# Attention of a decoder step: values' product as rounded 512-column passes, fused score step, reordered sample step

## The chip, the cores and the metric

One core of a Trainium2 chip. Time is device time in microseconds (us) of one execution; the kernel before has a median of 2323.82 us over 3 runs (2323.4 to 2323.91).

## The reference

One layer of a hybrid decoder for a prompt of 2048 tokens and for 8 sample rows with one token each. All arrays are float32, the width is 1024.

```python
proj = h @ w_in                       # h = x * (1 + scale) + shift
u_s, z_s, q, k, v, z_a, g_s, g_a = split(proj)
# prompt attention: blocks of 128 queries, keys of the own block and the one before
s = einsum('bnqkgd,bnskd->bnkgqs', qb, kk) * 64 ** -0.5 + rel_bias   # masked: -1e30
m = max(s.max(-1), sinks)
p = exp(s - m) / (exp(s - m).sum(-1) + exp(sinks - m))
o = einsum('bnkgqs,bnskd->bnqkgd', p, vv)
# sample attention: the same for one query per row against 128 cached keys and its own
...
b_a = (o * silu(z_a)) @ w_branch_a    # and an SSM branch b_s, a gated merge, w_out, LayerNorm
```

There are 16 heads of 64 and 4 key/value heads; four heads share one. `sinks` is one extra score per head that has no value.

## The kernel before

Every large product is done at nearly full precision with three passes of TensorE in a rounded float32 type (fp32r): each operand is split into a rounded high part and the low rest, and high x high, high x low and low x high are added (line 78). `products` goes through output blocks of 128 columns (jobs); a job is five chunks of the tokens (512, 256, 512, 264 and 512 columns in the order ORD), each with 24 matmuls into one of three PSUM accumulators `acc`. ScalarE copies an accumulator out (`zr`, L586) and writes it to DRAM (`zsD`, `gsD`, `gaD`).

Beside the jobs runs a side generator. A call after the third, sixth and eighth k of each chunk (a tick) issues its next piece. The instructions that result are put in order on each engine by the framework, which runs a model of the engines while it builds the program; each engine then works its queue in that order, and waits where an input or a buffer isn't ready.

The attention is such a side generator, beside 18 jobs. `attn_setup` (beside one job) writes the table of relative biases to DRAM (`biasD`, 3 MB, L894) and does the 8 sample rows: scores batch by batch (L924 transposes the cached keys, L930 multiplies), a softmax over 129 columns, transposes (L937, L938) and the product with the values: per batch a matmul over the 128 cached keys (L949) and one over the own key (L950), in one of four groups of 32 output columns (`tile_position`). `attn_blocks` (beside up to 17 jobs) runs 2 halves of the heads (P) x 16 blocks of 128 queries through a pipeline: a block starts each 7 ticks (`ii`) and goes through one stage per tick:

- `load` (SyncE's DMA queue), `conv` (splits q and k into high and low; q's parts lie above each other so that one pass does both);
- `scores` twice: matmuls into `ps` (L1034), then one VectorE step, score x 0.125 + bias, into `t1` (L1036);
- `soft` twice: row maximum (L868), with the sink (L869), negated (L871), exponential with a row sum on ScalarE (L876), sum, reciprocal, scaling (L881);
- `trans` twice: 8 transposes of p on TensorE into `pt` (L1048) and copies to SBUF (L1050);
- `pv` and `out`: o from float32 matmuls with 64-column weights of v (L1061), the halves e = 0 and 1 into partitions 0 to 63 and 64 to 127 of `po`; copy (L1068), times silu(z_a) on POOL (L1069), write to DRAM.

At the kernel's start the adaptive projection (L185) also works in column groups of 32, here with four groups taken in turn (0, 2, 1, 3).

PSUM has eight banks: three accumulators, two `ps`, two `pt`, one `po`. For a float32 matmul the trace has two records, for one in fp32r and for a transpose one. The next phase begins when all jobs are done.

Of the kernel before, what the change touches and what calls it, by code (L numbers as in the profile page):

```python
# [39 lines left out]
class Trunk:  # L40
# [842 lines left out]
    def attn_setup(self, p, pp):  # L883
# [7 lines left out]
        fr = p.tile([16, 384], F32, name="fr")  # L891
        nc.vector.memset(fr, NEG)
        nc.vector.tensor_copy(fr[:, 127:256], pr)
# [27 lines left out]
        for b in range(NS):  # L921
# [9 lines left out]
            yield  # L931
# [3 lines left out]
        yield  # L935
# [10 lines left out]
        for b in range(NS):  # L946
            i, n = divmod(b, 4)
            r = slice(32 * n, 32 * n + 32)
            nc.tensor.matmul(po[r, i], pT[:, b], vc[:, b], start=True, stop=False, tile_position=(0, 32 * n))  # L949
            nc.tensor.matmul(po[r, i], pl[:, b], vn[:, b], start=False, stop=True, tile_position=(0, 32 * n))  # L950
# [22 lines left out]
    def attn_blocks(self, p, pp, ii):  # L973
# [6 lines left out]
        sk = p.tile([128, 16], F32, name="skb", bufs=1)  # L980
        for P in range(2):
            v.tensor_copy(sk[:, 8 * P:8 * P + 8].rearrange("p (s i) -> p s i", s=2),
                          sn[:, 8 * P:8 * P + 8].rearrange("p (i s) -> p s i", s=2))
# [5 lines left out]
        def load(s):  # L989
            P, blk = s["P"], s["blk"]  # L990
            ts = slice(128 * blk, 128 * blk + 128)
            if blk == 0:
                bias = cur["bias"] = p.tile([128, 8, 384], F32, name="bias", bufs=1)
                for i in range(4):
                    for e in range(2):
                        src = self.biasD[8 * P + 2 * i + e, 127:127 + 383 * 128].rearrange("(i l) -> i l", l=383)
                        nc.sync.dma_start(bias[:, 4 * e + i, 0:256], src[:, 0:256])
                        nc.sync.dma_start(bias[:, 4 * e + i, 256:384], src[:, 0:128])
# [8 lines left out]
            vf = p.tile([128, 128], F32, name="vf", bufs=3)  # L1007
            nc.sync.dma_start(vf, self.vD[ts, P * 128:(P + 1) * 128])
            old = cur.get("v")
            s["v"] = (vf, old) if blk % 2 == 0 else (old, vf)  # L1010
            cur["v"] = vf
# [14 lines left out]
        def scores(s, e):  # L1026
            kw, qs = s["kw"], s["q"][e]
            b0 = 0 if s["blk"] % 2 else 128
            t1 = s["t", e] = p.tile([128, 4, 256], F32, name="t1", bufs=3)
            for g in range(2):  # L1030
                ps = pp.tile([128, 2, 256], F32, name="ps", bufs=2)
                for a2 in range(2):
                    for i, kk in enumerate((kh, kl)):
                        nc.tensor.matmul(ps[:, a2, kw], qs[:, 2 * g + a2], kk[:, g, kw], start=(i == 0), stop=(i == 1))  # L1034
                hd = slice(4 * e + 2 * g, 4 * e + 2 * g + 2)
                v.scalar_tensor_tensor(t1[:, 2 * g:2 * g + 2, kw], ps[:, :, kw], 0.125, s["bias"][:, hd, b0:b0 + kw.stop],  # L1036
                                       op0=OP.mult, op1=OP.add)

        def soft(s, e):
            mx = p.tile([128, 4], F32, name="mx")  # L1040
            g4 = 4 * (2 * s["P"] + e)
            self.softmax(p, s["t", e], mx, sk[:, g4:g4 + 4], 4, s["kw"])

        def trans(s, e):
            for h in s["hs"]:
                pt = pp.tile([128, 4, 128], F32, name="pt", bufs=2)
                for a in range(4):
                    nc.tensor.transpose(pt[:, a], s["t", e][:, a, h * 128:(h + 1) * 128], self.ident)  # L1048
                s["pT", e, h] = p.tile([128, 4, 128], F32, name="pT", bufs=4)
                nc.scalar.copy(s["pT", e, h], pt)  # L1050

        def pv(s):
            s["po"] = pp.tile([128, 4, 128], F32, name="po", bufs=1)
            s["z4"] = p.tile([128, 4, 128], F32, name="z4")
            nc.sync.dma_start(s["z4"], self.zaP[s["P"]][:, :, s["blk"] * 128:(s["blk"] + 1) * 128].rearrange("a p n -> p a n"))
            hs = s["hs"]
            for g in range(2):
                a = slice(2 * g, 2 * g + 2)
                for h in hs:
# [338 lines left out]
```

## Time and profile before

| | |
|---|---|
| median of 3 runs | 2323.82 us |
| the profiled execution | 2322.61 us, its span 2320.8 us |
| TensorE (PE) busy | 2271.6 us, 98% of the span |
| VectorE (DVE) | 1394.5 us, 60% |
| ScalarE (ACT) | 755.2 us, 33% |
| GpSimd (POOL) | 347.2 us, 15% |
| sample step | about 905 to 970 us from the span's start |
| attention blocks | about 985 to 1490 us |

Matmuls are pipelined: a record's duration is modelled and longer than the distance from one start to the next, which is what it costs. PEld is the weight load, which overlaps the matmuls. In a row, "idle before" is the time that the engine stood still ahead of the group, with what ended it.

### The profile page before, as it was taken

What the parts mean: (1) busy time and instruction counts of PE and PEld (TensorE: products, weight loads), DVE (VectorE), ACT (ScalarE), POOL (GpSimd) and SP (SyncE); (2) the same over time, 40 slices, a digit from 0 to 9 for tenths busy, and PEclk for the clock granted to TensorE, in tenths of its full rate; (3) what the DMA queues carried; (4) which work ended last, traced back from release to release, by engine and by line L of the source; (5) the groups of instructions that cost most, each with busy time, mean ns of one, the idle gap of its engine ahead of it and who ended that gap; (6) DMA issues with size and microseconds to landing.
All of it is one profiled execution on the core that took longest, in us unless ns stands there. A gap on an engine that the chain in (4) does not pass through costs nothing.

```text
span 2320.8 us, 34854 instructions
## 1 busy us (share of the span) xinstructions
PE 2271.6 (98%) x12819; PEld 1898.6 (82%) x12819; DVE 1394.5 (60%) x3100; ACT 755.2 (33%) x1636; POOL 347.2 (15%) x420
## 2 busy tenths in 40 slices
PE   7999999999999999999999999999999999999997
PEld 5888898888888888687877888887877888888886
DVE  4896229998888872167776666426446114224887
ACT  3411213331111211156676555435225113212100
POOL 1100001111112110000010000013552000222232
PEclk9999999999999999999999999999999999999999
DMA  9344623344434335633344333448337547667431
GB/s 293 104 150 127 202 77 113 110 124 117 117 115 119 115 112 129 132 105 110 103 140 116 91 105 111 114 111 221 116 103 241 148 124 219 197 183 239 147 114 65
DMA packets 387499, 317.97 MB, mean 137 GB/s; under 512 B 89334, under 2 KB 331406, under 8 KB 385743
## 3 DMA queue, kind: packets, MB, share of 16 engines
q1 hardware_dynamic: 349616, 260.28, 39.6%
q10 hardware_dynamic: 37712, 55.47, 7.0%
q8 instruction: 101, 1.65, 0.3%
q14 instruction: 70, 0.57, 0.1%
HBM read 195.24 MB, written 122.63 MB: 137 GB/s over the span
## 4 chain that ended last, share of the span: by engine, by line
PE 80%; DMA 8%; DVE 4%; SPq 3%; issue 2%; ACT 2%; POOL 1%; POOLq 0%; DVEq 0%; ACTq 0%
PE acc L78 56%; PE po L1332 7%; PE po L1061 3%; PE ps L1034 3%; PE pt L1048 2%; DMA z<-zsD 2%; PE acc L665 2%; DMA biasD<-fr 2%; PE xp L784 1%; PE yp L817 1%; PE yp L816 1%; SPq L178 1%; DVE sg L1197 1%; DMA xst<-ozP 1%; DMA xst<-ysD 1%
## 5 line engine op out<-in xcount | busy, mean ns | idle before, releaser
L78 PE MATMUL acc<-hh,whi 128*128 128x512 f32 (+2 forms) x2000 | 713.5, 357 | 0.1
L78 PE MATMUL acc<-hl,whi 128*128 128x512 f32 (+2 forms) x2000 | 703.6, 352 | 0.0
L78 PE MATMUL acc<-hh,wlo 128*128 128x512 f32 (+2 forms) x2000 | 701.8, 351 | 0.2 <-DVE wlo L59 0.2
L78 PEld LDWEIGHTS acc<-hh,whi 128*128 128x128 f32 x2000 | 377.3, 189 | 54.7 <-issue 8.5
L78 PEld LDWEIGHTS acc<-hl,whi 128*128 128x128 f32 x2000 | 377.5, 189 | 54.2 <-issue 8.0
L78 PEld LDWEIGHTS acc<-hh,wlo 128*128 128x128 f32 x2000 | 377.2, 189 | 52.1 <-issue 5.3
L78 PE MATMUL acc<-xh,whi 128*128 128x512 f32 (+2 forms) x960 | 335.9, 350 | 12.7 <-ACT sg L1192 10.4
L78 PE MATMUL acc<-xl,whi 128*128 128x512 f32 (+2 forms) x960 | 334.9, 349 | 1.9 <-DVE xl L1139 1.8
L78 PE MATMUL acc<-xh,wlo 128*128 128x512 f32 (+2 forms) x960 | 333.2, 347 | 0.0
L78 PEld LDWEIGHTS acc<-xh,whi 128*128 128x128 f32 x960 | 181.5, 189 | 41.1 <-ACT sg L1192 15.1
L78 PEld LDWEIGHTS acc<-xl,whi 128*128 128x128 f32 x960 | 181.4, 189 | 26.5 <-DVE xl L1139 4.0
L78 PEld LDWEIGHTS acc<-xh,wlo 128*128 128x128 f32 x960 | 181.3, 189 | 23.0
L59 DVE TENSOR_TENSOR wlo<-wst,whi 128x1024 fp32r<-128x1024 f32 x74 | 96.3, 1301 | 100.6 <-ACT whi L58 99.8
L1139 DVE TENSOR_TENSOR xl<-xst,xh 128x1024 fp32r<-128x1024 f32 (+2 forms) x84 | 104.2, 1257 | 81.3 <-ACT xh L1138 81.1
L876 ACT ACTIVATE t<-t,nm 128x256 f32<-128x256 f32 (+1 forms) x256 | 125.8, 495 | 33.0 <-DVE nm L871 30.2
L1036 DVE SCALAR_TENSOR_TENSOR t<-ps,bias 128x512 f32<-128x512 f32 (+1 forms) x128 | 81.8, 670 | 86.0 <-PE ps L1034 79.1
L58 ACT CAST whi<-wst 128x1024 fp32r<-128x1024 f32 x74 | 77.7, 1050 | 156.1 <-PE acc L78 140.6
L1069 POOL TENSOR_TENSOR o<-o,z 128x512 f32<-128x512 f32 x32 | 42.7, 1336 | 539.3 <-ACT o L1068 513.1
L1138 ACT CAST xh<-xst 128x1024 fp32r<-128x1024 f32 (+2 forms) x84 | 86.0, 1045 | 104.9 <-DMA xst<-mD 32.7
L586 ACT COPY zr<-acc 128x512 f32<-128x512 f32 (+2 forms) x120 | 59.9, 499 | 164.3 <-PE acc L78 132.1
L1332 PE MATMUL po<-wol,xh 128*128 128x512 f32 (+1 forms) x272 | 102.7, 377 | 0.8 <-DVE wol L1255 0.8
L1332 PE MATMUL po<-woh,xl 128*128 128x512 f32 (+1 forms) x272 | 102.6, 377 | 0.0
(355 smaller groups left out, 3277.8 us busy)
## 6 DMA issues: line engine op xcount, KB each, us to landing
wst<-in_w_in SPq DMA_DIRECT2D x50, 512.0 KB
uD<-u ACTq DMA_DIRECT2D x8, 1088.0 KB
u<-uD SPq DMA_DIRECT2D x32, 272.0 KB
yD<-y ACTq DMA_DIRECT2D x64, 132.0 KB
x<-in_x_prompt SPq DMA_DIRECT2D x16, 512.0 KB
wa<-in_w_ada SPq DMA_DIRECT2D x16, 512.0 KB
qf<-qD SPq DMA_DIRECT2D x32, 256.0 KB
z<-zaP SPq DMA_DIRECT2D x32, 256.0 KB
```

What stands on the lines that cost most here:

```text
L58: nc.scalar.copy(hi, st)
L59: nc.vector.tensor_tensor(lo, st, hi, op=OP.subtract)
L78: self.nc.tensor.matmul(ps[:, :n], w[:, k, :], x[:, k, :], start=(k == 0 and i == 0), stop=(k == KT - 1 and i == 2))
L586: nc.scalar.copy(z[:, :n], ps[:, :n])
L665: nc.tensor.matmul(ps[:mt, :256], x[:, k, ts], w[:, k, :], start=(i == 0), stop=(i == 23))
L876: nc.scalar.activation(t1[:, h, kw], t1[:, h, kw], AF.Exp, bias=nm[:, h:h + 1], accum_out=den[:, h:h + 1])
L1034: nc.tensor.matmul(ps[:, a2, kw], qs[:, 2 * g + a2], kk[:, g, kw], start=(i == 0), stop=(i == 1))
L1036: v.scalar_tensor_tensor(t1[:, 2 * g:2 * g + 2, kw], ps[:, :, kw], 0.125, s["bias"][:, hd, b0:b0 + kw.stop], op0=OP.mult, op1=OP.add)
L1061: nc.tensor.matmul(s["po"][e * 64:(e + 1) * 64, a], s["v"][h][:, g * 64:(g + 1) * 64], s["pT", e, h][:, a], start=(h == hs[0]), stop=(h == ...
L1138: nc.scalar.copy(xv(hi[:, k - 1:k + 1]), sv(st))
L1139: nc.vector.tensor_tensor(xv(lo[:, k - 1:k + 1]), sv(st), xv(hi[:, k - 1:k + 1]), op=OP.subtract)
L1332: nc.tensor.matmul(ps[:, :w], X[a][:, k, ts], Wo[h * w // 512][b][:, k, ws], start=(i == 0), stop=(i == 23))
```

## The change

The product with the values takes p as a rounded high and a low part (`ph`, `pl`) and v as high and low parts side by side in 128 weight columns (`vs`); a pass gives high rows in partitions 0 to 63 of `po` and low rows in 64 to 127, for all four heads of a key/value head at once (512 columns). A copy and two additions put them together in `o4`. The stages now go by key/value head (g) and not by half (e); the pipeline has twelve stages, `ii` stays 7. Score, bias and the row's maximum with the sink (as a minimum of the negated scores) are one VectorE instruction, `tensor_tensor_reduce`; its scale is -0.125, so the bias table is stored times 8 and the exponential has scale -1. In the sample step scores come two batches per tick, the softmax has four ticks, and the product goes over the four column groups in turn, all cached keys first and then the own ones.

```diff
         pr = pp.tile([16, 129], F32, name="pt", bufs=2)
         nc.tensor.matmul(pr, rb, oh, start=True, stop=True)
         fr = p.tile([16, 384], F32, name="fr")
+
         nc.vector.memset(fr, NEG)
-        nc.vector.tensor_copy(fr[:, 127:256], pr)
+        nc.vector.tensor_scalar(fr[:, 127:256], pr, 8.0, None, op0=OP.mult)
         nc.sync.dma_start(self.biasD.rearrange("h (r l) -> h r l", l=384), fr[:, None, :].to_broadcast([16, 128, 384]))
 
...
             for P in range(2):
                 i = b * 2 + P
                 nc.tensor.matmul(ss, qm[:, i * 128:(i + 1) * 128], kt[:, P], start=(i == 0), stop=(i == 15))
-            yield
+            if b % 2:
+                yield
         nc.vector.scalar_tensor_tensor(t1[:, 0], ss, 0.125, t1[:, 0], op0=OP.mult, op1=OP.add)
         mx = p.tile([128, 1], F32, name="mxs")
         self.softmax(p, t1, mx, sk, 1, slice(0, 129))
-        yield
+        for _ in range(4):
+            yield
...
         po = pp.tile([128, 2, 256], F32, name="po", bufs=1)
-        for b in range(NS):
-            i, n = divmod(b, 4)
-            r = slice(32 * n, 32 * n + 32)
-            nc.tensor.matmul(po[r, i], pT[:, b], vc[:, b], start=True, stop=False, tile_position=(0, 32 * n))
-            nc.tensor.matmul(po[r, i], pl[:, b], vn[:, b], start=False, stop=True, tile_position=(0, 32 * n))
+        yield
+        for i in range(2):
+            for pm, vm, first in ((pT, vc, True), (pl, vn, False)):
+                for n in range(4):
+                    b = 4 * i + n
+                    nc.tensor.matmul(po[32 * n:32 * n + 32, i], pm[:, b], vm[:, b], start=first, stop=not first,
+                                     tile_position=(0, 32 * n))
...
-        sk = p.tile([128, 16], F32, name="skb", bufs=1)
+        nsk = p.tile([128, 16], F32, name="skb", bufs=1)
         for P in range(2):
-            v.tensor_copy(sk[:, 8 * P:8 * P + 8].rearrange("p (s i) -> p s i", s=2),
-                          sn[:, 8 * P:8 * P + 8].rearrange("p (i s) -> p s i", s=2))
+            v.tensor_scalar(nsk[:, 8 * P:8 * P + 8].rearrange("p (g e a) -> p g e a", g=2, e=2),
+                            sn[:, 8 * P:8 * P + 8].rearrange("p (g a e) -> p g e a", g=2, e=2), -1.0, None, op0=OP.mult)
 
...
                     for e in range(2):
                         src = self.biasD[8 * P + 2 * i + e, 127:127 + 383 * 128].rearrange("(i l) -> i l", l=383)
-                        nc.sync.dma_start(bias[:, 4 * e + i, 0:256], src[:, 0:256])
-                        nc.sync.dma_start(bias[:, 4 * e + i, 256:384], src[:, 0:128])
+                        nc.sync.dma_start(bias[:, 4 * (i // 2) + 2 * e + i % 2, 0:256], src[:, 0:256])
+                        nc.sync.dma_start(bias[:, 4 * (i // 2) + 2 * e + i % 2, 256:384], src[:, 0:128])
...
             for h in range(2):
                 nc.sync.dma_start(s["kf"][h * 64:(h + 1) * 64], self.kD[P][:, ts].rearrange("(g d) n -> d g n", g=2))
-            vf = p.tile([128, 128], F32, name="vf", bufs=3)
-            nc.sync.dma_start(vf, self.vD[ts, P * 128:(P + 1) * 128])
-            old = cur.get("v")
-            s["v"] = (vf, old) if blk % 2 == 0 else (old, vf)
-            cur["v"] = vf
+            s["vf"] = p.tile([128, 2, 64], F32, name="vf", bufs=1)
+            nc.sync.dma_start(s["vf"], self.vD[ts, P * 128:(P + 1) * 128].rearrange("t (g d) -> t g d", g=2))
 
...
+            vs = p.tile([128, 2, 128], F32R, name="vs", bufs=3)
+            nc.scalar.copy(vs[:, :, 0:64], s["vf"])
+            v.tensor_tensor(vs[:, :, 64:128], s["vf"], vs[:, :, 0:64], op=OP.subtract)
+            old = cur.get("v")
+            s["v"] = (vs, old) if s["blk"] % 2 == 0 else (old, vs)
+            cur["v"] = vs
+
+        def scores(s, g):
+
+            kw = s["kw"]
             b0 = 0 if s["blk"] % 2 else 128
-            t1 = s["t", e] = p.tile([128, 4, 256], F32, name="t1", bufs=3)
-            for g in range(2):
+            t1 = s["t", g] = p.tile([128, 4, 256], F32, name="t1", bufs=3)
+            nm = s["nm", g] = p.tile([128, 4], F32, name="nm", bufs=3)
+            for e in range(2):
                 ps = pp.tile([128, 2, 256], F32, name="ps", bufs=2)
                 for a2 in range(2):
                     for i, kk in enumerate((kh, kl)):
-                        nc.tensor.matmul(ps[:, a2, kw], qs[:, 2 * g + a2], kk[:, g, kw], start=(i == 0), stop=(i == 1))
-                hd = slice(4 * e + 2 * g, 4 * e + 2 * g + 2)
-                v.scalar_tensor_tensor(t1[:, 2 * g:2 * g + 2, kw], ps[:, :, kw], 0.125, s["bias"][:, hd, b0:b0 + kw.stop],
-                                       op0=OP.mult, op1=OP.add)
-
-        def soft(s, e):
-            mx = p.tile([128, 4], F32, name="mx")
-            g4 = 4 * (2 * s["P"] + e)
-            self.softmax(p, s["t", e], mx, sk[:, g4:g4 + 4], 4, s["kw"])
-
-        def trans(s, e):
+                        nc.tensor.matmul(ps[:, a2, kw], s["q"][e][:, 2 * g + a2], kk[:, g, kw], start=(i == 0), stop=(i == 1))
+                for a2 in range(2):
+                    h = 2 * e + a2
+                    hs = 8 * s["P"] + 4 * g + h
+                    v.tensor_tensor_reduce(t1[:, h, kw], ps[:, a2, kw], s["bias"][:, 4 * g + h, b0:b0 + kw.stop], -0.125,
+                                           nsk[:, hs:hs + 1], OP.add, OP.min, nm[:, h:h + 1])
+
+        def soft(s, g):
+            kw, nm, t1 = s["kw"], s["nm", g], s["t", g]
+            hs = 8 * s["P"] + 4 * g
+            es = p.tile([128, 4], F32, name="es")
+            v.tensor_tensor(es, nm, nsk[:, hs:hs + 4], op=OP.subtract)
+            den = p.tile([128, 4], F32, name="den")
+            for h in range(4):
+                nc.scalar.activation(t1[:, h, kw], t1[:, h, kw], AF.Exp, bias=nm[:, h:h + 1], scale=-1.0,
+                                     accum_out=den[:, h:h + 1])
+            nc.scalar.activation(es, es, AF.Exp)
+            v.tensor_tensor(den, den, es, op=OP.add)
+            v.reciprocal(den, den)
+            for h in range(4):
+                v.tensor_scalar(t1[:, h, kw], t1[:, h, kw], den[:, h:h + 1], None, op0=OP.mult)
+
+        def trans(s, g):
+
             for h in s["hs"]:
                 pt = pp.tile([128, 4, 128], F32, name="pt", bufs=2)
                 for a in range(4):
-                    nc.tensor.transpose(pt[:, a], s["t", e][:, a, h * 128:(h + 1) * 128], self.ident)
-                s["pT", e, h] = p.tile([128, 4, 128], F32, name="pT", bufs=4)
-                nc.scalar.copy(s["pT", e, h], pt)
-
-        def pv(s):
-            s["po"] = pp.tile([128, 4, 128], F32, name="po", bufs=1)
-            s["z4"] = p.tile([128, 4, 128], F32, name="z4")
-            nc.sync.dma_start(s["z4"], self.zaP[s["P"]][:, :, s["blk"] * 128:(s["blk"] + 1) * 128].rearrange("a p n -> p a n"))
+                    nc.tensor.transpose(pt[:, a], s["t", g][:, a, h * 128:(h + 1) * 128], self.ident)
+                hi, lo = s["pT", h] = [p.tile([128, 4, 128], F32R, name=f"p{w}{h}", bufs=1) for w in "hl"]
+                nc.scalar.copy(hi, pt)
+                v.tensor_tensor(lo, pt, hi, op=OP.subtract)
+
+        def pv(s, g):
+
+            if g == 0:
+                s["z4"] = p.tile([128, 4, 128], F32, name="z4", bufs=1)
+                nc.sync.dma_start(s["z4"], self.zaP[s["P"]][:, :, s["blk"] * 128:(s["blk"] + 1) * 128].rearrange("a p n -> p a n"))
+                s["o4"] = p.tile([128, 4, 128], F32, name="o4", bufs=1)
+            po = pp.tile([128, 2, 2, 128], F32, name="po", bufs=1)
             hs = s["hs"]
-            for g in range(2):
-                a = slice(2 * g, 2 * g + 2)
-                for h in hs:
-                    for e in range(2):
-                        nc.tensor.matmul(s["po"][e * 64:(e + 1) * 64, a], s["v"][h][:, g * 64:(g + 1) * 64], s["pT", e, h][:, a],
-                                         start=(h == hs[0]), stop=(h == hs[-1]))
+            pr = po.rearrange("p e a q -> p (e a q)")
+            for h in hs:
+                for i, x in enumerate(s["pT", h]):
+                    nc.tensor.matmul(pr, s["v"][h][:, g], x.rearrange("p a q -> p (a q)"), start=(h == hs[0] and i == 0),
+                                     stop=(h == hs[-1] and i == 1))
+            tb = p.tile([64, 2, 2, 128], F32, name="tb", bufs=1)
+            nc.scalar.copy(tb, po[64:128])
+            for e in range(2):
+                v.tensor_tensor(s["o4"][64 * e:64 * e + 64, 2 * g:2 * g + 2], tb[:, e], po[0:64, e], op=OP.add)
 
         def out(s):
             P, blk = s["P"], s["blk"]
             ts = slice(blk * 128, (blk + 1) * 128)
-            o4 = p.tile([128, 4, 128], F32, name="o4")
-            nc.scalar.copy(o4, s["po"])
+            o4 = s["o4"]
             nc.gpsimd.tensor_tensor(o4, o4, s["z4"], op=OP.mult)
             nc.sync.dma_start(self.ozP[P][:, :, ts].rearrange("a p n -> p a n"), o4)
 
-        def s3(s):
-            scores(s, 1)
-            soft(s, 0)
-
-        def s7(s):
-            pv(s)
+        def s9(s):
+            pv(s, 0)
+            trans(s, 1)
+
+        def s11(s):
+            pv(s, 1)
             out(s)
 
-        stages = [load, conv, lambda s: scores(s, 0), s3, lambda s: soft(s, 1), lambda s: trans(s, 0),
-                  lambda s: trans(s, 1), s7]
+        def gap(s):
+            pass
+
+        stages = [load, conv, lambda s: scores(s, 0), lambda s: scores(s, 1), lambda s: soft(s, 0), lambda s: soft(s, 1),
+                  gap, lambda s: trans(s, 0), gap, s9, gap, s11]
         return self.pipeline([{"P": P, "blk": b} for P in range(2) for b in range(16)], stages, ii)
 
     def phase3(self, n2, n3, ii):
```

## Rows read from the trace of the kernel before

**Rows 1.** Stretches: window, length, busy us (count) of PE, PEld, DVE, ACT, POOL, clock, DMA.
```profile
900.00:985.00 85.00, 80.08 (x427) 63.62 (x426) 13.43 (x39) 14.35 (x32) 3.64 (x18) 0.98 0.67 141
985.00:1490.00 505.00, 505.00 (x3100) 405.44 (x3100) 347.43 (x877) 308.54 (x905) 41.44 (x31) 1.00 0.37 107
1490.00:1580.00 90.00, 90.00 (x489) 78.40 (x488) 29.48 (x20) 39.76 (x42) 11.26 (x7) 1.00 0.63 147
```

**Rows 2.** Chain of waits from 985 to 1490, shares by line.
```profile
by line: PE acc L78 60.3%; PE po L1061 15.8%; PE ps L1034 12.6%; PE pt L1048 11.4%
```

**Rows 3.** Groups by shape, TensorE, 985 to 1490: count, busy us, mean ns, idle before.
```profile
L1061 PE MATMUL po<-pT,vf 128*64 128x256 f32 x496 | 85.5, 393 | 0.0
```

**Rows 4.** Order in time, TensorE, attention and start: start us, us, instruction.
```profile
31.50 1.07 PE L185 MATMUL pm<-wa,c 128*32 128x128 f32 x30 [1.19 <-DMA wa<-in_w_ada]
...
1205.78 0.65 PE L1061 MATMUL po<-pT,vf 128*64 128x256 f32 x2
1206.36 0.39 PE L78 MATMUL acc<-hl,whi 128*128 128x264 f32 x1
...
1222.74 1.51 PE L1061 MATMUL po<-pT,vf 128*64 128x256 f32 x10
1224.18 0.55 PE L1048 MATMUL pt<-ident,t 128*128 128x128 f32 x3
...
1225.49 0.40 PE L78 MATMUL acc<-hh,whi 128*128 128x512 f32 x1
1225.72 0.39 PE L78 MATMUL acc<-hl,whi 128*128 128x512 f32 x1
```

**Rows 5.** Chain of waits in the sample step: start us, us, engine, line.
```profile
909.65 36.02 DMA biasD<-fr
...
955.26 0.55 PE po L949 x2
...
963.46 0.54 PE po L950 x2
```

**Rows 6.** Order in time, TensorE, sample step.
```profile
914.81 0.60 PE L924 MATMUL pt<-ident,kc 128*128 128x128 f32 x4
...
920.04 1.05 PE L930 MATMUL po<-kts,qm 128*128 128x129 f32 x8
...
948.47 0.45 PE L937 MATMUL pt<-ident,t1s 128*128 128x128 f32 x1 [4.92 <-DVE t1s L881]
```

**Rows 7.** Order in time, ScalarE, sample step.
```profile
944.67 0.59 ACT L586 COPY zr<-acc 128x512 f32<-128x512 f32 x1 [6.69 <-DMA zsD<-zr]
...
945.72 1.28 ACT L876 ACT_TABLE_LOAD   x1 [0.46 <-DMA biasD<-fr]
```

**Rows 8.** Groups by shape, VectorE, 985 to 1490.
```profile
L1036 DVE SCALAR_TENSOR_TENSOR t<-ps,bias 128x512 f32<-128x512 f32 x120 | 78.7, 686 | 78.0 <-PE ps L1034 77.9
...
L868 DVE TENSOR_REDUCE mx<-t 128x4 f32<-128x1024 f32 x60 | 73.2, 1219 | 1.6
...
L1024 DVE TENSOR_TENSOR kl<-kf,kh 128x256 fp32r<-128x256 f32 x32 | 14.5, 454 | 2.1 <-ACT kh L1023 2.0
L869 DVE TENSOR_TENSOR mx<-mx,skb 128x4 f32<-128x4 f32 x64 | 12.3, 192 | 1.4
...
L871 DVE TENSOR_SCALAR nm<-mx 128x4 f32<-128x4 f32 x64 | 10.7, 167 | 1.4
...
L1036 DVE SCALAR_TENSOR_TENSOR t<-ps,bias 128x256 f32<-128x256 f32 x8 | 3.1, 420 | 7.9 <-DMA bias<-biasD 3.5 <-issue 3.2 <-PE ps L1034 1.2
```

**Rows 9.** Groups by shape, ScalarE, 985 to 1490.
```profile
L876 ACT ACTIVATION_READ_ACCUMULATOR t<-t,nm 128x1 f32 x256 | 48.7, 190 | 0.0
...
L1017 ACT CAST q<-qf 64x512 fp32r<-64x512 f32 x31 | 19.3, 622 | 31.0 <-PE ps L1034 25.4 <-DMA qf<-qD 3.4 <-DMA gsD<-zr 2.1
```

**Rows 10.** Waits of VectorE, 985 to 1490: total us, times, longest.
```profile
DVE t L1036 <- PE ps L1034: 79.1, 57, 5.2
DVE den L878 <- ACT es L877: 40.9, 31, 3.2
```

More of the change, by code (lines that the diff above doesn't have):

```diff
@@ L1024, in conv @@
             v.tensor_tensor(kl[:, :, h], kf, kh[:, :, h], op=OP.subtract)
-        def scores(s, e):
-            kw, qs = s["kw"], s["q"][e]
+            vs = p.tile([128, 2, 128], F32R, name="vs", bufs=3)
[6 more added lines that the diff above has]
+            kw = s["kw"]
             b0 = 0 if s["blk"] % 2 else 128
-            t1 = s["t", e] = p.tile([128, 4, 256], F32, name="t1", bufs=3)
-            for g in range(2):
+            t1 = s["t", g] = p.tile([128, 4, 256], F32, name="t1", bufs=3)
+            nm = s["nm", g] = p.tile([128, 4], F32, name="nm", bufs=3)
+            for e in range(2):
                 ps = pp.tile([128, 2, 256], F32, name="ps", bufs=2)
```

## The prediction

> **What bounds the kernel now.** Three views, in this order. The table of stretches first: in the attention stretch (985 to 1490 us) TensorE is busy for all of 505 us, VectorE for 347 (69%), ScalarE for 309 (61%); in the stretch ahead of it (900 to 985) TensorE lacks 4.9 us [rows 1]. So the attention stretch is worth what TensorE's work leaves it, as long as no other engine becomes late, and the one before has a hole. Then the chain of waits over the attention stretch: it is TensorE alone, and the values' product (L1061) has 15.8% of it [rows 2], 0.158 x 505 = 79.8 us. Last the groups by shape and the order in time, for the prices.
>
> **Values' product on TensorE.** Before: 496 records (248 products of 128x256, two records each; the two 64-column halves alternate) [rows 3], so 79.8 / 496 = 0.161 us a record. Ten in a row take 1.44 us (1222.74 to 1224.18), 0.144 each; two alone take 0.58 (1205.78 to 1206.36), 0.29 each [rows 4]: the halves run two at a time, and a short group pays for going in and out. After: 62 block halves x 2 groups x 2 passes (high and low part of p) = 248 passes of 128x512 in the rounded type on 128-column weights. That is the form of L78, whose starts lie 0.23 us apart (1225.49 to 1225.72) [rows 4]: 248 x 0.23 = 57.0 us. Gain 79.8 - 57.0 = 22.8. Unknown is how often a change of form is still paid: the excess of a pair, 0.58 - 0.29 = 0.29 us, for some 20 of the 64 calls is 6 us either way, so 17 to 29. Scores (L1034) and transposes (L1048) keep form and count.
>
> **Sample step, its product.** Sixteen pairs of records stand one behind the other, 0.55 us each, from 955.26 to 964.00: 8.7 us [rows 5]. Neighbours use the same column group there; after the change four groups follow each other. The adaptive projection already runs in such an order: 30 records of 128x128 in 1.07 us, 0.036 each [rows 4]; for 256 columns twice that, 0.071 x 32 = 2.3 us. Gain 6.4. If only two run at a time, as in L1061 (32 x 0.144 = 4.6), it is 4.1. I take 6.4.
>
> **Sample step, the hole.** At 948.47 TensorE has waited 4.92 us for VectorE's softmax result t1s [rows 6]. The cause shows on ScalarE: the copy `zr` at 944.67 had waited 6.69 us for its buffer, whose write to zsD stood behind the 36.02 us write of biasD [rows 5, 7], and the exponential was queued behind that copy, with a table load of 1.28 us of its own. The change issues two batches of scores a tick instead of one and leaves four ticks between softmax and transposes; if the exponential gets ahead of these copies, the wait for t1s goes. What is late next: the same copies free the accumulators, of which there are three. The one copied at 944.67 is free at 945.26, 1.7 us after TensorE stopped (948.47 - 4.92 = 943.55), so about that much stays. Gain 4.9 - 1.7 = 3.2, taken as 3; bounds 0 (the whole hole moves to the accumulators) and 4.9. The scores, the softmax and the POOL fills of this step stay what they are, and no DMA of it is added or moved past another. The scaling of fr by 8 rides in a copy that was there.
>
> **VectorE.** Gone, by the groups of the stretch [rows 8]: score and bias 78.7 + 3.1, row maximum 73.2, its two small steps 12.3 + 10.7: 178.0 us. New:
> - 256 fused steps (score + bias + minimum) on 128x256. The trace has no such operation. Nearest is score and bias at 128x256 out of PSUM, 0.420 us: 107.5. This is the low end. High end: the minimum is read out by an instruction of its own, priced as the smallest steps, 0.167: 256 x 0.167 = 42.8 more.
> - 124 subtractions for the low part of p, 128x512 out of PSUM, as 0.686: 85.1.
> - 128 additions into o4, 64x256, as 0.420: 53.8.
> - 32 subtractions for v, 128x128, at most kl's 0.454: 14.5.
>
> Sum 260.9, or 303.7 with reads; net +83 or +126. VectorE goes from 347 to 430 or 473 in a stretch that shrinks to 505 - 23 = 482 us: 89% or 98%. TensorE's work hides it; the cover left is 52 us or 9. I take the high end, since ScalarE's 256 exponentials with a row sum each have such a read behind them, 0.190 us [rows 9].
>
> The Trainium skill's page "VectorE: DVE Perf Modes", section "Two Vector instructions with no wait between them", counts a VectorE operation that also writes out its accumulator as two instructions, the second an accumulator read, and so speaks against the change. No run of before shows it on VectorE. By the page the VectorE sum is the 473, by the fused row alone the 430.
>
> VectorE runs in order, and today it waits 79.1 us for scores and 40.9 for exponentials [rows 10], at no cost. For what these waits cost in a nearly full queue I take 6 us of TensorE idle. Why so little: the new stages leave two ticks between transpose, product and addition, and the order on the queues isn't tied to the ticks but laid out by a planner. The code has one batch of scores a tick (8 products); the trace has two at a time (L924 x4, L930 x8), with 914.81 to 920.04 between them [rows 6], which is some 21 products at 0.23. Where the planner expects VectorE to be full it can spread the blocks over the products that today follow the stretch (1490 to 1580: TensorE 90 of 90 us busy, VectorE 29 [rows 1]).
>
> **ScalarE.** The copies of p stay 124, now rounding. The copy of po becomes 64 copies of 64x512, as 0.622 [rows 9]: 40 us; v's rounding is at most 32 x 0.622 = 20. With nothing taken off for the old copy 309 + 60 = 369 of 482, 77%: hidden.
>
> **Waits added.** o4 and z4 have one buffer each now. The z4 load moves two stages back and must wait on SP for POOL's product of the block before; that ended five ticks earlier (5/7 of 505 / 32 = 11 us), so nothing queues behind it. The additions wait for the ozP write of the block before, issued at the same point; behind a late one all of VectorE would stand. vf's load, which waited for the values' product, now waits only for a conversion one tick on: SP gets looser. All at nothing.
>
> **Sum.** Against the profiled execution (2322.61 us, span 2320.8; the median of the runs, 2323.82, lies 1.2 above): -22.8 - 6.4 - 3 + 6 = -26.2, so 2296.4 there and 2297.6 by the median. Predicted: 2297.
>
> **Rivals.**
> - VectorE becomes the bound (slower). Place: fused steps and low parts in the attention stretch. With reads (473) and half of today's 120 us of waits unfilled the stretch takes 533 us instead of 482: 2297 - 6 + 51 = 2342. It decides where VectorE's busy time and unfilled waits pass 482 + 32 = 514. For: 98% leaves an in-order queue no room. Against: most waits are there because VectorE has nothing else to do, and the blocks can spread. Chance 0.16.
> - The same, milder: the stretch takes 505 to 520, which gives back the product's gain: 2297 - 6 + 23 = 2314 to 2329. Chance 0.13.
> - The hole stays as a wait for accumulators: 2300. Chance 0.11.
> - VectorE costs nothing, and the changes of form go too: -29 - 6.4 - 4.9 = -40: 2283. Chance 0.06.
>
> The forecast has 0.54; its own range is 2287 to 2309 (product 17 to 29, sample step 4 to 11, idle 0 to 12).
>
> **How the numbers follow.** A difference that can be told from none here is 0.2%, 4.6 us, so the same is 2319 to 2328. Faster: 0.54 + 0.11 + 0.06 + 0.04 of the milder case = 0.75; same 0.08; slower 0.16 + 0.01 = 0.17. The range runs from the best case, 2283, to 2325 inside the milder one; nearly all that it leaves out is the first rival.
>
> **What would show it.** Right: 248 records 128x512 at the values' product, 0.23 us apart; the sample product in some 2.3 us; no wait for t1s above 2 us; TensorE idle in the stretch below 12 us with VectorE 85 to 98% busy. Wrong: TensorE waits of over 30 us in sum for ps, pt or the low part of p, released by VectorE; a fused step well above 0.6 us with its read; passes spaced well over 0.23.

## The result and the profile after

The changed kernel takes 2282.88 us (median of 4 runs, 2280.57 to 2284.62) against 2323.86 us for the kernel before on the same chip: ratio 0.9817, 95% interval 0.9805 to 0.9829. The profiled executions are 2281.77 and 2322.61 us, 40.8 apart; 26.2 were forecast. The table of stretches of the changed kernel, columns as in [rows 1]:

```profile
900.00:985.00 85.00, 79.85 (x468) 67.81 (x467) 16.64 (x52) 16.82 (x41) 3.62 (x18) 0.98 0.71 154
985.00:1470.00 485.00, 485.00 (x2934) 426.92 (x2933) 417.03 (x1342) 342.46 (x967) 42.10 (x32) 1.00 0.38 112
1470.00:1580.00 110.00, 106.67 (x565) 91.01 (x564) 57.39 (x50) 58.75 (x65) 28.62 (x21) 1.00 0.79 194
```

TensorE is busy for all of the attention stretch, which now ends at 1470 (1490 before); VectorE rose from 69 to 86% of it. The chain of waits over this stretch is still TensorE alone, with less of the values' product (L1061 before, L1088 now) than in [rows 2]:

```profile
by line: PE acc L78 64.8%; PE ps L1045 12.2%; PE po L1088 11.9%; PE pt L1072 11.2%
```

Order in time on TensorE, with the sample's transpose first:

```profile
948.01 0.45 PE L940 MATMUL pt<-ident,t1s 128*128 128x128 f32 x1 [5.15 <-DVE t1s L881]
...
1201.44 0.40 PE L1088 MATMUL po<-ph,vs 128*128 128x512 f32 x1
1201.67 0.40 PE L1088 MATMUL po<-pl,vs 128*128 128x512 f32 x1
1201.91 0.40 PE L1088 MATMUL po<-ph,vs 128*128 128x512 f32 x1
1202.14 0.29 PE L78 MATMUL acc<-hl,whi 128*128 128x264 f32 x1
...
1202.98 0.60 PE L1072 MATMUL pt<-ident,t 128*128 128x128 f32 x4
1203.33 0.36 PE L1045 MATMUL ps<-kh,q 128*128 128x256 f32 x1
```

The passes start 0.23 us apart, as forecast; the hole of [rows 6] is still there, 5.15 us for 4.92. The chain through the sample step (answers to [rows 5]: 2.27 us where 8.7 stood) and ScalarE's order there ([rows 7]):

```profile
909.08 36.17 DMA biasD<-fr
...
954.83 2.27 PE po L954 x32
```
```profile
936.76 0.37 ACT L586 COPY zr<-acc 128x256 f32<-128x256 f32 x1 [8.46 <-DMA zsD<-zr]
...
944.22 0.58 ACT L586 COPY zr<-acc 128x512 f32<-128x512 f32 x1 [7.09 <-DMA zsD<-zr]
...
945.27 1.28 ACT L876 ACT_TABLE_LOAD   x1 [0.46 <-DMA biasD<-fr]
```

Groups by shape on VectorE, 985 to 1470 (answers to [rows 8]), and its waits there ([rows 10]):

```profile
L1049 DVE CUSTOM_DVE_ANT_0 t<-ps,bias,skb 128x256 f32<-128x256 f32 x240 | 104.7, 479 | 2.3 <-PE ps L1045 1.4
L1075 DVE TENSOR_TENSOR pl<-pt,ph 128x512 fp32r<-128x512 f32 x124 | 85.0, 687 | 16.4 <-ACT ph L1074 14.7 <-PE po L1088 0.2
...
L1093 DVE TENSOR_TENSOR o<-tb,po 64x256 f32<-64x256 f32 x128 | 52.6, 411 | 16.0 <-ACT tb L1091 9.1 <-issue 3.4 <-DMA ozP<-o 2.3
...
L1049 DVE DVE_READ_ACCUMULATOR2_ANT nm<- 128x1 f32 x253 | 20.9, 82 | 0.0
```
```profile
DVE den L1062 <- ACT es L1061: 19.8, 36, 1.3
...
DVE t L1049 <- PE ps L1045: 1.4, 5, 0.4
```

VectorE's 79.1 us of waiting for scores shrank to 1.4: the new work went into waits it already had.

**Where the time went.** I summed the distances from one TensorE start to the next by line, from the sample's last product (965 before, 958 after) to the end of the jobs beside the attention (1570.2 and 1526.6): 605.1 us became 568.6. The values' product gives 21.5 of the 36.5 (79.6 to 58.1). The other 15 come from lines whose form and count did not change: transposes 53.0 to 43.0, scores 65.0 to 63.4, the jobs' products 407.2 to 403.7. (Part of the transposes' 10 only moves between lines: the last of a group hands on 0.08 us early, the instruction behind it takes 0.08 more, and there are 135 groups where there were 84.) TensorE waits for nothing in either stretch. Ahead of these stretches the sample product gives 6.5. The phases behind give back 2.8; their waits for `sg`, `xh` and `xl` went from 14.2 to 17.1 us, and runs of one kernel differ by as much. The 15 can be seen in the order of the kernel before:

```profile
1180.16 0.60 PE L1048 MATMUL pt<-ident,t 128*128 128x128 f32 x4
1180.52 0.48 PE L78 MATMUL acc<-hh,wlo 128*128 128x512 f32 x1
1180.84 0.40 PE L78 MATMUL acc<-hh,whi 128*128 128x512 f32 x1
1181.16 0.65 PE L1061 MATMUL po<-pT,vf 128*64 128x256 f32 x2
1181.74 0.66 PE L1048 MATMUL pt<-ident,t 128*128 128x128 f32 x4
1182.15 0.48 PE L78 MATMUL acc<-hl,whi 128*128 128x512 f32 x1
1182.47 0.39 PE L78 MATMUL acc<-hh,wlo 128*128 128x512 f32 x1
1182.70 0.40 PE L78 MATMUL acc<-hh,whi 128*128 128x512 f32 x1
```

Four transposes take 0.36 us between full-width neighbours and 0.41 behind the 64-column product, and that product's own two records 0.58. The jobs' product right ahead of it (1180.84) takes 0.32 us to the next start, where 0.23 is usual (1182.47). Over all 84 groups of the half-width product, and against the same line and shape elsewhere in the stretch, the instruction ahead takes 0.104 us more, 8.7 us in all, and the one behind 0.092 more, 6.8 us: 15.5 us that the neighbours pay.

### The profile page after: what moved, and what is told of

The parts are those of the page before. It is cut to its first block, busy times and chain, and to the rows that moved or that the text cites. A ratio compares the mean times of both kernels' runs of the same rounds, so it can differ in the third digit from the quotient of the medians.

```text
span 2280.0 us, 35059 instructions
## 1 busy us (share of the span) xinstructions
PE 2228.8 (98%) x12571; PEld 1904.1 (84%) x12571; DVE 1464.8 (64%) x3576; ACT 786.9 (35%) x1700; POOL 349.7 (15%) x420
## 4 chain that ended last, share of the span: by engine, by line
PE 80%; DMA 9%; DVE 4%; SPq 3%; issue 2%; ACT 1%; POOL 1%; POOLq 0%; DVEq 0%; ACTq 0%
PE acc L78 57%; PE po L1365 7%; DMA z<-zsD 3%; PE ps L1045 3%; PE po L1088 3%; PE pt L1072 2%; PE acc L665 2%; DMA biasD<-fr 2%; PE xp L784 1%; PE yp L817 1%; PE yp L816 1%; SPq L178 1%; DVE sg L1230 1%; DMA xst<-ozP 1%; DMA xst<-ysD 1%
## 5 line engine op out<-in xcount | busy, mean ns | idle before, releaser
L1049 DVE CUSTOM_DVE_ANT_0 t<-ps,bias,skb 128x256 f32<-128x256 f32 (+1 forms) x256 | 109.7, 470 | 5.9 <-issue 3.1
L1365 PE MATMUL po<-woh,xh 128*128 128x512 f32 (+1 forms) x272 | 102.6, 377 | 0.0
```

What stands on the lines that cost most here:

```text
L1049: v.tensor_tensor_reduce(t1[:, h, kw], ps[:, a2, kw], s["bias"][:, 4 * g + h, b0:b0 + kw.stop], -0.125, nsk[:, hs:hs + 1], OP.add, OP.min, ...
L1365: nc.tensor.matmul(ps[:, :w], X[a][:, k, ts], Wo[h * w // 512][b][:, k, ws], start=(i == 0), stop=(i == 23))
```

## The experiments

Ratios are to the kernel before; "below" and "above" are medians. The kernel before was timed on the same chip each time. The changed kernel was measured again beside experiment 1 and the first run of experiment 6: 2283.66 us, 0.9821 [0.9808, 0.9835].

**1. Is the change of form a cost by itself?** The old half-width product is put back in miniature: one 64-column matmul ahead of each of the 64 products, in one run on half of the array's columns, in the other (the control) on all.

```diff
             pr = po.rearrange("p e a q -> p (e a q)")
+            nc.tensor.matmul(pr[64:128, 0:64], self.ident[:, 0:64], self.ident[:, 0:64], start=True, stop=True)  # narrow
+            nc.tensor.matmul(pr[:, 0:64], self.ident, self.ident[:, 0:64], start=True, stop=True)                # wide
```


> Changed kernel, with one float32 product of 64 columns on 64 output columns (partitions 64 to 127 of po) ahead of each of the 64 value products; its result is overwritten. Theory (half-width float32 products make the products, transposes and scores beside them dearer; leaving them is the 15 us that the prediction's sum lacks): 64 changes of form at about 0.25 us each on top of the product's own cost, so 15 us or more above the run with the full-width product beside it, and transposes that cost more than 0.088 us each. Rival (the 15 us come from the new order of the stages, which keeps transposes in groups of four): within 4 us of the full-width run.

> Changed kernel, with one float32 product of 64 columns on all 128 output columns ahead of each of the 64 value products; its result is overwritten. It is the control for the half-width run: two records of 64 columns and one change between float32 and the rounded type, some 0.1 to 0.3 us a call by both theories, 6 to 20 us above the changed kernel.

Narrow: 2312.08 us, 0.9939 [0.9927, 0.9952]. Wide: 2297.68, 0.9878 [0.9865, 0.9892]. Order on TensorE, narrow and then wide:

```profile
1205.23 0.33 PE L1086 MATMUL po<-ident 128*64 128x64 f32 x2
1205.49 0.50 PE L1089 MATMUL po<-ph,vs 128*128 128x512 f32 x1
```
```profile
1206.54 0.33 PE L1086 MATMUL po<-ident 128*128 128x64 f32 x2
1206.68 0.48 PE L1089 MATMUL po<-ph,vs 128*128 128x512 f32 x1
```

The same columns take 0.26 us narrow and 0.14 wide from start to start. The runs differ by 14.4 us, just under the 15 that I expected: 0.225 for each of 64 excursions to half width and back. Of that 0.12 stands on the inserted records; the instruction ahead of the insert takes 0.094 us more than elsewhere in the narrow run and 0.006 in the wide one, the one behind 0.105 and 0.085. So what the neighbour ahead paid in the kernel before (0.104 each, 8.7 of the 15 us) is the change of form. What the one behind paid (6.8) is mostly not: it also stands behind a float32 product of full width, and went because the new product is fp32r. The Trainium skill's page "TensorEngine Tiling (Array Packing)", section "Key Properties", says that a change of the tiling mode drains TensorE; these runs agree, with 0.094 us ahead of the narrow insert, and put 0.225 us on the whole excursion for float32.

**2. Is VectorE near its limit?** The score step and the maximum apart again, all else changed.

```diff
-                for a2 in range(2):
-                    v.tensor_tensor_reduce(t1[:, h, kw], ps[:, a2, kw], ..., nm[:, h:h + 1])
+                v.scalar_tensor_tensor(t1[:, 2 * e:2 * e + 2, kw], ps[:, :, kw], 0.125, ...)   # and softmax() as before
```


> The changed kernel with the score step taken apart again: one scale-and-bias operation per two heads, and the maximum, its combination with the sink and the shift as the kernel before has them; everything else stays changed. VectorE then has about 50 us more to do in the attention stretch, 467 of 485 us in place of 417. Theory (TensorE's own list of products sets the time, the planner spreads the blocks, and VectorE is not waited for until it is nearly full): within 5 us of the changed kernel, 2278 to 2288 us, and TensorE idle in the attention stretch stays under 3 us. Rival (VectorE is what the change leaned on, and the fused step pays for the changed product): 2298 us or more, with TensorE waiting for t or for the low part of the probabilities.

2334.1 us, 1.0034 [1.0021, 1.0046]: slower than the kernel before, 50 above the changed one. My theory fell. The rival's price came, but not its sign. Stretches, and the additions into `o4` by line:

```profile
985.00:1470.00 485.00, 485.00 (x2895) 426.81 (x2893) 404.21 (x992) 300.61 (x851) 34.65 (x26) 1.00 0.36 107
1470.00:1500.00 30.00, 30.00 (x180) 26.29 (x179) 25.24 (x63) 19.95 (x58) 1.42 (x1) 1.00 0.35 106
1500.00:1560.00 60.00, 36.93 (x180) 27.53 (x178) 42.03 (x108) 31.13 (x82) 6.47 (x5) 0.83 0.36 90
```
```profile
L1080 DVE TENSOR_TENSOR o<-tb,po x128: 381/414/417, 1004.1 to 1550.2; 64x256 f32<-64x256 f32 x128
```

TensorE waits for nothing until 1500, and VectorE is busy for less of the stretch (404) than in the changed kernel (417). But a block comes every 17.1 us ((1550.2 - 1004.1) / 32; 14.7 in the changed kernel, whose additions run from 997.8 to 1469.4): the queues were laid out with more of the jobs' products between the blocks, these ran out at about 1500, and the last blocks ran uncovered, TensorE idle for 23 of the 60 us from 1500 to 1560, at a mean granted clock of 0.83 (about a third of the stretch at the 1.2 GHz level).

**3. Busy time, or something else?** VectorE work that nothing reads, added to the changed kernel: one such operation per softmax, or three.

```diff
+            for h in range(1):     # or 3
+                xx = p.tile([128, 192], F32, name="xx", bufs=1)
+                v.tensor_scalar(xx[:, w], t1[:, h, w], 0.5, None, op0=OP.mult)
```


> The changed kernel with one more VectorE operation per softmax of four heads: 192 of the columns of one head scaled into a tile that nothing reads, 64 in all at an estimated 0.28 us, so some 18 us on VectorE in the attention stretch (435 of 485 us), and nothing added to any chain. Theory A (VectorE was near its limit already in the changed kernel: the run without the fused step lost 50 us because it gave VectorE 50 us more): 2283 to 2300 us, most of the 18 us still fitting. Theory B (that loss came from the longer chain of the separate maximum, shift and exponentials, not from busy time): within 2 us of the changed kernel.

> The same with three such operations, 192 at 0.28 us, some 54 us: as much VectorE time as the fused step saves, put where it lengthens no chain. Theory A (busy time): 2320 to 2340 us, the last attention sums late by 50 us or more, TensorE out of other products by then. Theory B (the separate maximum's chain): 2283 to 2295 us.

One: 2284.75, 0.9818 [0.9801, 0.9835]. Three: 2290.25, 0.9843 [0.9827, 0.9859]. Three in the table of stretches:

```profile
985.00:1470.00 485.00, 483.49 (x2902) 422.34 (x2901) 446.84 (x1532) 339.09 (x964) 40.21 (x30) 1.00 0.38 111
```

VectorE at 92% costs 6 us. But the records of these operations, 50.1 us in sum, partly overlap with others: over the whole execution VectorE's busy time rose from 1464.8 to 1500.0 us, 35 more, where experiment 2 has 1511.7, 47 more. Three quarters of that busy time cost an eighth of the 50 us, so busy time alone hardly explains experiment 2; no run excludes that the last quarter would cost far more.

**4. What holds the blocks back?** Four edits of the run of experiment 2: the maximum per two heads behind each score step; the softmax's second half a tick later; a block each 6 ticks; four buffers of `t1` (with a bias tile of 256 columns, so that even blocks add the bias of the wrong keys).

```diff
+                v.tensor_reduce(mx[:, 2 * e:2 * e + 2], t1[:, 2 * e:2 * e + 2, kw], ...)   # e11: in scores
-    ... lambda s: soft(s, 0), lambda s: soft(s, 1), gap, ...
+    ... lambda s: soft_a(s, 0), s5, lambda s: soft_b(s, 1), ...                           # e10
-            self.phase3(n2, n3, 7)
+            self.phase3(n2, n3, 6)                                                        # e12
-            t1 = s["t", g] = p.tile([128, 4, 256], F32, name="t1", bufs=3)
+            t1 = s["t", g] = p.tile([128, 4, 256], F32, name="t1", bufs=4)                # e13
```


> The run without the fused step again, with one edit: the row maximum is taken per two heads right behind each score step, where the fused step has it, and not in one piece of 1.2 us at the head of the softmax. VectorE's busy time stays that of the run without the fused step (some 470 us). Theory (the fused step's worth is mostly that the maximum is there early, so that VectorE's fixed order meets fewer waits for exponentials and scores): 2290 to 2312 us, against 2334 without the edit and 2290 for the changed kernel with as much idle work added. Rival (the place of the maximum doesn't matter; what the fused step gives is fewer and shorter pieces in the queue's order as a whole): 2326 to 2340 us.

> The run without the fused step again, with another edit: the softmax is cut in two stages, and sum, reciprocal and scaling come one tick after the exponentials. VectorE waited 38.5 us for exponentials in the run without the edit and 19.8 in the changed kernel. Theory (these waits stand in a queue that is nearly full, and no work is laid into them): with a tick between, the wait for exponentials falls below 20 us and the time to 2300 to 2318 us. Rival (the order on the queues is laid out by dependences and not by ticks, so the cut changes nothing): 2328 to 2340 us.

> The run without the fused step again, with a block started every 6 ticks in place of 7. In that run TensorE is busy all through the stretch but takes on a block only every 17 us (14.7 in the changed kernel), and runs out of the jobs' products before the attention ends. Theory (the blocks are held by what they need, a buffer of t1 or VectorE, not by the ticks): nothing is gained, 2328 to 2340 us. Rival (the ticks set the blocks' pace): blocks come about 2 us sooner each, 2285 to 2310 us.

> The run without the fused step again, with four buffers of t1 in place of three. The room comes from the bias tile, 256 columns wide in place of 384: the blocks of even number then add the bias of the wrong key columns, and 16 loads of 64 KB fall away. In the run without the fused step VectorE waited 20.2 us, 20 times, for the transposes that free a buffer of t1; in the changed kernel it never did. Theory (with the maximum apart a t1 lives longer, and three of them hold the blocks to one every 17 us): blocks every 15 us, 2285 to 2305 us, and that wait gone. Rival (VectorE's busy time with the waits in its own order holds the blocks): 2320 to 2336 us, with VectorE waiting elsewhere.

In this order: 2328.71 us, 1.0006 [0.9996, 1.0016]; 2334.5, 1.0031 [1.0019, 1.0042]; 2334.82, 1.0039 [1.0026, 1.0051]; 2316.67, 0.9961 [0.9948, 0.9975]. The early maximum gives 5 us, the later half and the ticks nothing; the fourth buffer gives 17 of the 50, between my two forecasts, with a block each 16.5 us. Waits of VectorE in the run of experiment 2 and with four buffers:

```profile
DVE den L878 <- ACT es L877: 38.5, 24, 2.2
DVE t L1046 <- PE pt L1059: 20.2, 20, 2.2
```
```profile
DVE den L878 <- ACT es L877: 24.3, 17, 2.2
DVE t L1045 <- PE pt L1058: 13.4, 9, 2.8
```

With the maximum apart a `t1` lives longer, and a score step waits for the transposes (`pt`) to free one; the changed kernel has no such wait. So about a third of the fused step's worth is a buffer that turns over sooner, if the 16 loads that this run also leaves out count for nothing; the wait fell from 20.2 to 13.4 us only, so it can be more. The rest stays open: busy time, waits for exponentials and the laid-out order act together there, and no run takes one of them alone.

**5. The other parts alone**, in the kernel before: the fused step, and the sample step.

> The kernel before with the fused score step alone, the values' product left in its float32 form of half width. VectorE gets some 50 us of work less. Theory (TensorE is the bound and does not wait for VectorE): within 3 us of the kernel before, transposes still 0.11 us each. Rival (part of the unpredicted 15 us comes from a shorter chain on VectorE): 5 to 10 us below the kernel before, with the transposes or the scores cheaper.

> The kernel before with the reordered sample step alone. Theory: the values' product of the sample falls from 8.7 to 2.3 us and the hole before its weights' transpose stays at about 5 us, so 6 to 7 us below the kernel before, 2317 us. Rival (the reordering also closes the hole, and the changed kernel's hole has another cause): 10 to 12 us below, 2312 us, with the wait before L940's transpose under 2 us. Rival (neither is on the path): within 2 us of the kernel before.

Fused step: 2325.41, 1.0000 [0.9991, 1.0009]. VectorE had slack in the kernel before, so some 55 us of its work (288 us busy from 985 to 1470, 343 with the sample step alone) were worth nothing there. Sample step: 2318.08, 0.9965 [0.9951, 0.9979], 7.5 below; the hole is there, and the product is as short as in the changed kernel. The stretch with the fused step, then with the sample step, and of the latter the order on TensorE and the chain of waits:

```profile
985.00:1470.00 485.00, 485.00 (x2976) 388.80 (x2976) 287.83 (x1048) 302.40 (x886) 39.51 (x30) 1.00 0.37 109
```
```profile
985.00:1470.00 485.00, 485.00 (x2982) 389.23 (x2981) 343.32 (x871) 303.08 (x895) 40.94 (x31) 1.00 0.36 106
```

```profile
949.88 0.44 PE L940 MATMUL pt<-ident,t1s 128*128 128x128 f32 x1 [6.32 <-DVE t1s L881]
```
```profile
956.88 2.27 PE po L954 x32
```

**6. The hole.** Moving the bias table's write behind the softmax changed nothing, since nothing tied it there and it was issued at 911 as before: 2281.61, 0.9809 [0.9796, 0.9823], hole 4.99.

> Changed kernel, with the 3 MB write of the bias table issued behind the sample step's softmax instead of ahead of its loads. Theory (the hole of 5 us is that write's doing: it holds back the writes of zsD, these the copies on ScalarE, these the exponential): the hole ahead of the transposes of the softmax is gone, the time 4 to 6 us below the changed kernel. Rival (the write holds back the copies wherever it stands, and TensorE then waits for an accumulator or the next weights): a hole of 3 us or more some 10 to 30 us later, no gain over 2 us.

Two halves of 8 heads, the second tied to the softmax:

> The changed kernel with the 3 MB write of the bias table in two halves: the first pair's 8 heads where the whole write stands, the second pair's behind the sample's softmax, on which it is made to depend. Theory (the hole before the sample's transpose is the exponential queued on ScalarE behind copies of zr, and these wait for writes that the bias table's write holds up): the first half takes about 18 us, the copies of zr no longer wait 7 to 8.5 us, the hole falls from 5 us to under 1, and the kernel comes 4 to 6 us below the changed one, 2278 us. Rival (the hole is the sample chain's own length, or it only moves to the accumulator): within 2 us of the changed kernel. Rival on the other side: the second half collides with the first blocks' loads, 3 us or more above.

2303.8, 0.9905 [0.9892, 0.9919], and a hole of 5.7 us. The first half, from 8 partitions, still took until about 948 (issued at 910.5): the DMA share from 912 to 945 was 0.56 where it is 0.92, so half the bytes took as long. The second half then held SP's queue, and the blocks' bias loads went out at 986.7 instead of 956.6. The rival on the other side came. With the first half spread over 16 partitions and the second in slices:

> The changed kernel with the bias table's first half (8 heads) written from 16 partitions, two per head with 64 rows each, so that all 16 DMA engines share it, and the second half in eight slices beside the loads of blocks 2 to 9. Theory (the copies of zr, and with them the exponential, wait for the 36 us write): that write takes about 18 us, the copies at 936 and 944 no longer wait 7 us and more, the hole before the sample's transpose falls below 1 us, 2277 to 2280 us against 2283. Rival (other traffic of that stretch, the caches' and the weights' loads, holds the copies up): the copies still wait, the hole stays at 5 us, within 2 us of the changed kernel. Rival on the other side (the slices delay the blocks' loads): over 2286 us.

2283.72, 0.9814 [0.9795, 0.9833]. Seven of the eight slices were issued before 935, so the stretch kept its traffic (share 0.95), and the hole split: 3.37 us for an accumulator, 1.11 for the softmax.

```profile
941.23 0.50 PE L78 MATMUL acc<-hh,whi 128*128 128x512 f32 x1 [3.37 <-ACT zr L586]
...
950.34 0.30 PE L948 MATMUL pt<-ident,t1s 128*128 128x128 f32 x1 [1.11 <-DVE t1s L881]
```

Last, one row per head in place of 128, which every partition of the bias tile then loads (not in the cut below); the query's offset in the bias is left out:

```diff
-        nc.sync.dma_start(self.biasD.rearrange("h (r l) -> h r l", l=384), fr[:, None, :].to_broadcast([16, 128, 384]))
+        nc.sync.dma_start(self.biasD[:, 0:384], fr)
```


> The changed kernel with one row per head written to the bias table in place of 128, and every partition of the bias tile loaded from that row: the step of the bias from query to query is left out, and with it the 3 MB write. Loads, their sizes and everything behind them stay. Theory (that write holds up the writes of zr, hence ScalarE's copies, hence the exponential and the accumulators): no wait of 7 us and more for zr's buffers, the hole before the sample's transpose under 1 us and no other wait of TensorE in its place, 4 to 6 us below the changed kernel, 2277 to 2279 us against 2283. Rival (the caches' and the weights' loads are enough to hold them up): a hole of 3 us or more, here or at the accumulators, within 2 us of the changed kernel.

2286.68, 0.9833 [0.9820, 0.9847]. The hole is gone, with the copies' waits: TensorE is busy for 33.00 of 33 us from 912 to 945, 30.86 in the changed kernel. The write is its cause. But TensorE then waits, 7.6 us in all and most of it where the blocks of each half of the heads start (981 and 1227 to 1238), and the time is not below the changed kernel's:

```profile
945.81 0.27 PE L940 MATMUL pt<-ident,t1s 128*128 128x128 f32 x1
```
```profile
PE ps L1046 <- ACT kh L1026: 4.7, 2, 3.4
```

What the hole gave was lost there, at the second half by the run's own loads: all partitions read one row, a packet of 1 KB there took 84 ns on the mean for 56, and VectorE waited 4.4 us for the bias. So what a closed hole is worth stays open. No variant beat the changed kernel clear of noise.

## Why the prediction was right or wrong

| term | forecast | measured |
|---|---|---|
| values' product, on its own records | -22.8 | -21.5 |
| on the product's neighbours | 0 (changes of form: 6 either way) | -15.0 |
| sample product | -6.4 | -6.5 |
| hole | -3 | +0.2 |
| TensorE idle for VectorE | +6 | none |
| phases behind | 0 | +2.8 |
| sum | -26.2 | -40.0 of -40.8 |

- **The step that failed** is the change of form, "the excess of a pair, 0.58 - 0.29 = 0.29 us, for some 20 of the 64 calls is 6 us either way". I looked for it only on the product's records and in a third of the calls, and put what its neighbours pay at nothing ("Scores (L1034) and transposes (L1048) keep form and count"). They gave 15.0 us (15.5 by the distances next to the product): 8.7 stood ahead of 84 half-width groups and is the change of form (experiment 1: 0.094 us ahead of a narrow insert, 0.006 ahead of a wide one); 6.8 stood behind them and goes mostly with a float32 product of any width, a term that I didn't have at all. The rows that showed it were in the trace of before: the same four transposes in 0.36 and 0.41 us, the jobs' product in 0.23 and 0.32.
- **VectorE** had two errors in its price: the fused step takes 0.479 us for 0.420, its read 0.082 for 0.167. The Trainium skill's page "VectorE: DVE Perf Modes", section "Two Vector instructions with no wait between them", was right that there is such a read (253 in the stretch); at 20.9 us in all it is half of my bound. VectorE came to 417 of 485 us, below both of my figures, and in experiment 3 even 447 cost only 6 us. "For what these waits cost in a nearly full queue I take 6 us of TensorE idle" was too much.
- **The rival "VectorE becomes the bound"** named a real mechanism and a near price (2342; 2334 measured), but for the change without its fused step. Its sign was wrong: I looked for TensorE waiting in the stretch, and it shows as fewer blocks per time and idle time behind the stretch. That the blocks can spread, which I held against this rival, is how it costs.
- **The hole.** The cause was read rightly (experiment 6 removes it with the write), the remedy was not: the exponential stayed queued behind the copies, since the new ticks did not change the order on ScalarE (table load at 945.27; 945.72 in [rows 7]).
- The rival "VectorE costs nothing, and the changes of form go too: 2283" has the number that came, by luck: the product and its neighbours gave 36.5 us where it has 29, and that made up for the hole, which did not close (4.9), and for the phases behind (2.8).

## What to carry to other kernels

When a matmul of another array shape goes, count the changes of form around it and look at the neighbours' distances, ahead and behind, not only at its own records. Parts of a change don't add: the fused step was worth nothing alone (experiment 5) and 50 us under the new product (experiment 2), because only there VectorE, with its waits and buffers, set the pace of the blocks. Where a planner lays out the queues, a late engine shows as work thinned out and cover used up early, so compare the pace of the blocks and the stretch behind, not waits.

## What the runs showed of the hardware

- A float32 matmul of half width among full-width ones costs 0.225 us more than one of full width with the same columns (14.4 us for 64): 0.12 on its own records, 0.09 on the instruction ahead, 0.02 on the one behind.
- The instruction behind a float32 matmul of either width takes 0.085 to 0.105 us longer than elsewhere (experiment 1).
- The fused step on VectorE, which has an accumulator output, has a second instruction of 82 ns behind it; the one behind ScalarE's exponentials takes 190 [rows 9].
- Four column groups of 32 in turn: 32 records in 2.27 us, 0.071 each, against 8.7 us when neighbours share a group.
- A 1.5 MB write from 8 partitions took about as long (37 us) as 3 MB from 16 (36 us), at a DMA share of 0.56 against 0.92.
